# Queueing the S5 share behind the block's own work in the first stage of a hybrid encoder

## The chip, the cores and the metric

The kernel runs on one core of one Trainium2 chip. A core has a matrix engine (TensorE, PE in the rows), VectorE (DVE), ScalarE (ACT), GpSimd (POOL) and SyncE (SP); the last issues DMAs and computes nothing. Each engine takes its instructions in the order in which they stand in its own queue and waits on semaphores for the others. The metric is device time in microseconds (us) of one execution: the median of three runs before is 2523.85 us (2522.33 to 2524.93).

## The reference, cut to what matters

One layer, float32, on 3072 positions of width 1024 (one sequence of 1024, one of 2048):

```python
h = rmsnorm(x, norm_g)
u_a, v_a, z_a, x_b, z_b = split(h @ w_in)                 # five blocks of 1024 columns
y_a = gelu(u_a) * (w_s @ layernorm(gelu(v_a)) + b_s) * silu(z_a)       # chunks of 128 positions
y_b = S5 scan of x_b, forward and backward, 64 groups of 16 channels, 64 complex states each
y_b = glu(gelu(y_b + d_skip * x_b)) * silu(z_b)
out = rmsnorm(x + concat(y_a, y_b) @ w_out, final_g)
```

The S5 scan needs, for every group, matrices that come from the parameters alone (powers of the discretised state factor times the input and output maps). The kernel works these out itself: that is the "S5 setup".

## The kernel before, in words

Every float32 product is made of three passes over split operands (`mm3`, L57 to L61: high by high, high by low, low by high), so a block of 128 output columns by 512 positions is 24 matmuls of 512 columns.

**First stage (L204 to L365).** It makes x_b transposed, for three row groups `th` of 1024 positions. For each of them it runs 16 blocks: 8 weight columns times two halves of 512 positions, 48 blocks in all. A block is 24 matmuls `mm<-h..,whl` and then, in `xb_op`, one ScalarE copy of PSUM into the tile `xo` (L329); every second block SyncE sends `xo` out. After each block `after()` runs what else is due:

- a step of the norm of a coming half (`norm_half`). Its first step loads four tiles `x` of 128 rows, squares them on ScalarE (L267), works out the scale on tiny VectorE tiles (L269, and L48 to L53) and scales the four tiles on VectorE (L275). Each of the next eight steps is four TensorE transposes (`tr`, L283), a ScalarE copy `hf` (L285) and two VectorE passes, a cast and a subtraction (L287, L288), that leave a split tile of the half (`hx..`, `ha..`, `hb..`). A half has eight such tiles.
- from the third block on, a share of `s5_setup`. Blocks 3, 5, 7, 9 and 10 (the list `S5AT`, L34) take its head. From block 11 on every block takes one share: `build` of one pair of groups (32 pairs) and then `finish` of the pair before it.

A share's `build(gp)` (L953) is on VectorE two products, a difference and a scaled difference (`m`, `m`, `pc`, `pc`: L967, L968, L970, L972) and two products and a difference (L989, L990, L991: `pb`). GpSimd does the two products for the second `pc` (L967, L968), three operations for the second `pb` (L989 to L991) and four small copies into one of two tiles `Bm` (L997). ScalarE's queue issues four DMAs `mat_d<-pc` (L975). The share's `finish(gp - 1)` (L1000) is on TensorE four products into the PSUM tile `s5b` (L1007, eight rows in the trace) and four transposes into `s5a` (L1020). ScalarE copies `s5b` into `ksb` (L1010, L1011) and `s5a` into `pbt` (L1022). VectorE adds into `ksb` (L1012, the last reader of `s5b`) and finishes it (L1015, twice). ScalarE's queue sends both out (L1016, L1023). There is one `s5b` tile, so the `finish` of a pair can only start on TensorE when L1012 of the pair before is done.

Between blocks ScalarE and GpSimd also split the next weights `whl` (L151, L152: two halves for every weight, and a weight serves two blocks).

**The order.** The kernel is written in Python and a scheduler orders it when the program is built: it takes instructions by priority (the order of the text, moved by `tc.high_priority`) as soon as its own estimate says that their inputs are there, and puts them on the engines in that order. An instruction that the estimate finds ready may so be put ahead of older ones that are not. `with tc.issue_after(i.ins)` forbids that against one instruction: whatever is traced inside the block and goes to the same engine as `i` stands behind `i` in that engine's queue. It adds no wait across engines. The kernel uses it already for the first share of the setup, which is put behind the first half's scaling and copy:

```python
if blocks == S5AT[0]:
    with tc.issue_after(pin["x"].ins), tc.issue_after(pin["h"].ins):
        next(s5)
elif blocks in S5AT or blocks > S5AT[-1]:
    next(s5, None)
```

**Later stages (L368 on).** The second stage makes the other four column blocks, mixes branch A, and runs the 64 S5 groups in shares; the last two make the GLU and the output projection. Nothing in them is edited.

Of the kernel before, what the change touches and what calls it, by code (L numbers as in the profile page):

```python
# [11 lines left out]
F32 = mybir.dt.float32  # L12
# [4 lines left out]
ALU = mybir.AluOpType  # L17
# [16 lines left out]
S5AT = (3, 5, 7, 9, 10)  # L34
# [9 lines left out]
def newton_rsqrt(nc, pool, v, n, tag):  # L44

    y = pool.tile([P, n], F32, tag=tag + "y", name=tag + "y")
    a = pool.tile([P, n], F32, tag=tag + "a", name=tag + "a")
    nc.vector.tensor_scalar(y.bitcast(I32), v.bitcast(I32), -0.5, 1597463007.0,  # L48
                            op0=ALU.mult, op1=ALU.add)
    for _ in range(3):  # L50
        nc.vector.tensor_tensor(a, y, y, op=ALU.mult)
        nc.vector.scalar_tensor_tensor(a, a, -0.5, v, op0=ALU.mult, op1=ALU.mult)
        nc.vector.scalar_tensor_tensor(y, a, 1.5, y, op0=ALU.add, op1=ALU.mult)  # L53
    return y
# [9 lines left out]
def hybrid_encoder(ctx, tc, a, outs):  # L64
    nc = tc.nc
    V, S, G, T = nc.vector, nc.scalar, nc.gpsimd, nc.tensor
# [115 lines left out]
    def sweep(pool, half, ops, after, hp=WHP):  # L182

        ws = [ready.pop(0) for _ in ops]
        for jh in range(2):
            for w, f in zip(ws, ops):
                ps = pool.tile([P, 512], F32, tag="mm", name="mm")
                h = half(jh)
                for kt in range(KT):
                    mm3(nc, ps, w[:, 0, kt], w[:, 1, kt], h[kt][:, 0], h[kt][:, 1], kt == 0, kt == KT - 1)  # L190
                if jh:
                    next_w(hp)
                f(jh, ps)
                after()

    def by_j(t, jh):

        return t[:, :, 64 * jh:64 * jh + 64]

    def cols(t):  # L200
        return t.rearrange("p (k j) -> p j k", j=J)


    with ExitStack() as p1:  # L204
# [46 lines left out]
        pin = {}  # L251

        def norm_half(hf):


            th, jh = hf // 2, hf % 2
            ss = small.tile([P, 4], F32, tag="ss", name="ss")
            xs = []
            for c in range(4):
                if hf == 1:  # L260
                    x = hpool.tile([P, D], F32, tag=f"hb{c}", name="x")
                else:
                    x = xpool.tile([P, D], F32, tag="x", name="x")
                dma(x, x_src[th][P * (4 * jh + c):P * (4 * jh + c) + P])
                junk = xpool.tile([P, D], BF16, tag="junk", name="junk", bufs=1)
                with tc.issue_after(pin["h"].ins) if hf == 1 else ExitStack():
                    S.activation(junk, x, AF.Square, accum_out=ss[:, c:c + 1])  # L267
                xs.append(x)
            V.tensor_scalar(ss, ss, 1.0 / D, EPS, op0=ALU.mult, op1=ALU.add)  # L269
            rs = newton_rsqrt(nc, small, ss, 4, "rx")  # L270
            for c in range(4):
                if hf == 0 and c == 3:
                    pin["x0"] = S.activation(xs[c], xs[c], AF.Copy, scale=rs[:, c:c + 1])
                else:
                    pin["x"] = V.tensor_scalar(xs[c], xs[c], rs[:, c:c + 1], None, op0=ALU.mult)  # L275
            yield
            pool, tag = ((h1pool, "x"), (hpool, "a"), (hpool, "b"))[hf % 3]
            halves[hf] = []
            for kt in range(KT):
                h = pool.tile([P, 2, 512], F32R, tag=f"h{tag}{kt}", name=f"h{tag}{kt}")  # L280
                pt = ps_tr.tile([P, 512], F32, tag="tr", name="tr")
                for c in range(4):
                    T.transpose(pt[:, P * c:P * c + P], xs[c][:, P * kt:P * kt + P], ident)  # L283
                hf32 = xpool.tile([P, 512], F32, tag="hf", name="hf32", bufs=HFB)
                i = S.activation(hf32, pt, AF.Copy, scale=NG[:, kt:kt + 1])  # L285
                pin.setdefault("h", i)
                V.tensor_copy(h[:, 0], hf32)  # L287
                V.tensor_tensor(h[:, 1], hf32, h[:, 0].bitcast(F32), op=ALU.subtract)  # L288
                halves[hf].append(h)
                if hf < 4:  # L290
                    dma(hs_d[hf, kt], hf32)
                yield

        def steps(gen, n):
            for _ in range(n):
                next(gen, None)

        with tc.high_priority():
            n0 = norm_half(0)
            steps(n0, 1)  # L300

            stage_next()
            col = order.pop(0)[2]
            two = [hpool.tile([P, 512], F32, tag=f"hb{6 + i}", name="wf") for i in range(2)]
            src = w_in[:, col:col + P].rearrange("(kt p) c -> p kt c", p=P)
            for i in range(2):
                pin["w"] = dma(two[i].rearrange("p (a c) -> p a c", c=P), src[:, 4 * i:4 * i + 4])
            staged.append((None, two, lambda w: w))

            with tc.issue_after(pin["x0"].ins):  # L310
                split_w(1000)
                split_w(1000)
            steps(n0, 8)
        with tc.issue_after(pin["w"].ins):
            n1 = norm_half(1)
            steps(n1, 1)
            stage_next()
        s5 = s5_setup(p1, tc, a, xpool, ps_s5, ident, kio, f8h, f8l, r8, ks_d, mat_d)
        blocks = 0
# [3 lines left out]
        for th in range(NTH):  # L323
            xos = {}

            def xb_op(fb, jh, ps):
                if not jh:
                    xos[fb] = xpool.tile([P, J, P], F32, tag="xo", name="xo", bufs=2)
                S.copy(by_j(xos[fb][:, ::-1], jh), cols(ps))  # L329
                if jh:  # L330
                    dma(xb_d[P * fb:P * fb + P, :, P * th:P * th + P], xos[fb])

            def after():

                nonlocal blocks, n1, n2, n3
                i = blocks % 16
                if i < 2:
                    steps(n1, 2 if th else 4)
                if th < NTH - 1:
                    if i == 2:  # L340
                        n2 = norm_half(2 * th + 2)
                        steps(n2, 1)
                    if 4 <= i < 12:
                        steps(n2, 1)
                    if i == 12:
                        n3 = norm_half(2 * th + 3)
                        steps(n3, 1)
                    if i >= 14:
                        steps(n3, 2)
                    if i == 15:  # L350
                        n1 = n3
                blocks += 1
                if blocks == S5AT[0]:
                    with tc.issue_after(pin["x"].ins), tc.issue_after(pin["h"].ins):
                        next(s5)
                elif blocks in S5AT or blocks > S5AT[-1]:
                    next(s5, None)
                if blocks >= S5AT[-1]:
                    next(mx, None)

            for fbs in ((0, 1), (2,), (3,), (4,), (5,), (6, 7)):
                sweep(ps_mm, lambda jh: halves[2 * th + jh], [lambda *x, fb=fb: xb_op(fb, *x) for fb in fbs], after,
                      XHP if blocks else 0)
# [4 lines left out]
    with ExitStack() as p2:  # L368
# [8 lines left out]
        s5 = s5_groups(tc, spool, ps_b, small, kio, f8h, f8l, r8, xb_d, ks_d, mat_d, gy_d)  # L377
# [837 lines left out]
```

## Time and profile before

| what | value |
|---|---|
| median of three runs | 2523.85 us |
| profiled execution, its own time | 2522.37 us |
| its span, first to last instruction | 2520.6 us |
| TensorE busy | 2440.8 us, 97% of the span |
| VectorE busy | 1750.4 us, 69% |
| ScalarE busy | 976.7 us, 39% |
| GpSimd busy | 622.5 us, 25% |
| mean granted TensorE clock | 0.991 |
| first to last `xo` copy (the first stage's blocks) | 36.2 to 395.7 us |

The profiled execution took 1.8 us more than its span, and lies 1.5 us under the median. The shares of the whole span mix stages. The first stage is told apart by windows of time: in them "busy" of TensorE counts overlapping matmuls, so a window that reads 12.00 of 12.00 has no gap on TensorE, and what is missing to the window's length is time in which it waited.

### The profile page before, as it was taken

To read this page: it belongs to the slowest core of one execution; us is meant where nothing else is said; L and a number is where in the kernel's file an instruction comes from. 1 tells how busy PE (TensorE), PEld (TensorE's weight loads), DVE (VectorE), ACT (ScalarE), POOL (GpSimd) and SP (SyncE) were. 2 spreads that over 40 slices of the span, in tenths; PEclk is the share of its full clock that TensorE was granted. 3 is DMA by queue.
4 is the path that set the end of the run, shared out by engine and by line. 5 is a ranking of instruction groups with operands and counts; after the bars stand their busy time and mean duration, and the time that the engine had idled before them with its cause. 6 is when DMAs were issued, how large, how long until landed. Compare 5 with 4: busy or idle time off the path is not lost.

```text
span 2520.6 us, 34031 instructions
## 1 busy us (share of the span) xinstructions
PE 2440.8 (97%) x12313; PEld 2077.6 (82%) x12313; DVE 1750.4 (69%) x2921; ACT 976.7 (39%) x1738; POOL 622.5 (25%) x623
## 2 busy tenths in 40 slices
PE   7999999989999899999999999999999999999998
PEld 5777779978888798888889888887888888888886
DVE  6888856899999969888887989755455533333332
ACT  5343334445554534444454454424343411111110
POOL 1579873344334302210130231101000100000000
PEclk9999999999999999999999999999999999999999
DMA  8565455355555533544453444456465732222220
GB/s 240 171 190 146 143 161 192 115 170 175 177 181 190 179 100 122 153 157 149 135 177 119 127 132 150 135 168 179 135 183 160 234 109 92 92 96 93 96 76 30
DMA packets 363017, 367.21 MB, mean 146 GB/s; under 512 B 40768, under 2 KB 308576, under 8 KB 350560
## 3 DMA queue, kind: packets, MB, share of 16 engines
q1 hardware_dynamic: 311008, 343.99, 43.3%
q10 hardware_dynamic: 51840, 21.04, 3.4%
q8 instruction: 97, 1.59, 0.3%
q14 instruction: 72, 0.59, 0.1%
HBM read 229.76 MB, written 135.20 MB: 145 GB/s over the span
## 4 chain that ended last, share of the span: by engine, by line
PE 72%; DVE 12%; DMA 3%; issue 1%; POOL 1%; ACT 0%; SPq 0%; ACTq 0%; DVEq 0%; POOLq 0%
PE mm L59 20%; PE mm L61 20%; PE mm L60 19%; PE acc L59 2%; PE acc L60 2%; PE acc L61 2%; DVE gt L1121 2%; PE py L59 1%; PE py L61 1%; PE py L60 1%; PE sv L498 1%; DVE h L1127 1%; DMA hf<-hs_d 1%; PE pb L59 1%; PE pb L61 1%
## 5 line engine op out<-in xcount | busy, mean ns | idle before, releaser
L59 PE MATMUL mm<-w,yh 128*128 128x512 f32 x768 | 302.6, 394 | 0.0
L60 PE MATMUL mm<-w,yh 128*128 128x512 f32 x768 | 301.8, 393 | 0.0
L61 PE MATMUL mm<-w,yh 128*128 128x512 f32 x768 | 301.3, 392 | 0.0
L59 PE MATMUL mm<-ha,whl 128*128 128x512 f32 x704 | 277.7, 395 | 9.9 <-DVE v L503 9.6
L59 PE MATMUL mm<-hb,whl 128*128 128x512 f32 x704 | 277.5, 394 | 6.8 <-DVE v L503 6.8
L61 PE MATMUL mm<-ha,whl 128*128 128x512 f32 x704 | 275.6, 391 | 1.1 <-POOL whl L152 1.1
L61 PE MATMUL mm<-hb,whl 128*128 128x512 f32 x704 | 275.6, 391 | 0.0
L60 PE MATMUL mm<-ha,whl 128*128 128x512 f32 x704 | 275.4, 391 | 0.0
L60 PE MATMUL mm<-hb,whl 128*128 128x512 f32 x704 | 275.3, 391 | 0.0
L152 POOL TENSOR_TENSOR whl<-wf,whl 128x512 fp32r<-128x512 f32 x112 | 176.2, 1591 | 226.1 <-ACT whl L151 197.4
L1121 DVE TENSOR_TENSOR_SCAN gt<-dec,b 64x768 f32<-64x768 f32 x128 | 229.8, 1795 | 3.1
L1057 POOL TENSOR_TENSOR mi<-m,mi 128x256 fp32r<-128x256 f32 x64 | 59.7, 933 | 530.3 <-ACT mi L1056 530.3
L61 PEld LDWEIGHTS mm<-w,yh 128*128 128x128 f32 x768 | 144.3, 188 | 33.8
L59 PEld LDWEIGHTS mm<-w,yh 128*128 128x128 f32 x768 | 144.0, 188 | 33.2
L60 PEld LDWEIGHTS mm<-w,yh 128*128 128x128 f32 x768 | 144.0, 187 | 33.1
L700 DVE SCALAR_TENSOR_TENSOR yh<-yf,yh 128x512 fp32r<-128x512 f32 x96 | 66.8, 699 | 148.4 <-ACT yh L699 115.2
L59 PEld LDWEIGHTS mm<-ha,whl 128*128 128x128 f32 x704 | 132.9, 189 | 36.9 <-DVE v L503 10.4
L729 DVE TENSOR_TENSOR xr<-xr,mm 128x512 f32<-128x512 f32 x48 | 33.0, 688 | 184.1 <-PE mm L61 184.1
L59 PEld LDWEIGHTS mm<-hb,whl 128*128 128x128 f32 x704 | 133.1, 189 | 32.8 <-DVE v L503 7.7
L61 PEld LDWEIGHTS mm<-ha,whl 128*128 128x128 f32 x704 | 132.7, 188 | 29.4 <-POOL whl L152 1.6
L61 PEld LDWEIGHTS mm<-hb,whl 128*128 128x128 f32 x704 | 132.9, 189 | 27.9
L60 PEld LDWEIGHTS mm<-ha,whl 128*128 128x128 f32 x704 | 132.8, 189 | 25.9 <-DVE ha L288 0.4
(243 smaller groups left out, 5942.3 us busy)
## 6 DMA issues: line engine op xcount, KB each, us to landing
whl<-wc_d SPq DMA_DIRECT2D x64, 1024.0 KB
wc_d<-whl SPq DMA_DIRECT2D x32, 1024.0 KB
wf<-in_w_in_dram SPq DMA_DIRECT2D x112, 256.0 KB
m<-mat_d SPq DMA_DIRECT2D x128, 128.0 KB
xb_d<-xo SPq DMA_DIRECT2D x24, 512.0 KB
U<-xb_d SPq DMA_DIRECT2D x64, 192.0 KB
gy_d<-gy SPq DMA_DIRECT2D x64, 192.0 KB
zb_d<-zb SPq DMA_DIRECT2D x24, 512.0 KB
```

The source lines that it names most:

```text
L59: nc.tensor.matmul(out, lh, rh, start=first, stop=False)
L60: nc.tensor.matmul(out, lh, rl, start=False, stop=False)
L61: nc.tensor.matmul(out, ll, rh, start=False, stop=last)
L152: G.tensor_tensor(flat[:, 1, sl], wf, flat[:, 0, sl].bitcast(F32), op=ALU.subtract)
L498: T.matmul(sv[:, db], h[:, 0, dsl], w, start=True, stop=False)
L700: V.scalar_tensor_tensor(y[:, 1], yf, sc, y[:, 0].bitcast(F32), op0=ALU.mult, op1=ALU.subtract)
L729: V.tensor_tensor(x, x, t.ps[i], op=ALU.add)
L1057: eng.tensor_tensor(t[:, 1], src, t[:, 0].bitcast(F32), op=ALU.subtract)
L1121: V.tensor_tensor_scan(o[r, f], dec[r, f], bf[r, f], 0.0, op0=ALU.mult, op1=ALU.add)
L1127: V.tensor_tensor(h2, gt[:, ::-1], sn, op=ALU.mult)
```

## The change: what it does

From the eleventh block on, the share is traced under two `issue_after`: one for the last VectorE instruction of the block's own norm work (`pin["V"]`: a scaling L275 or a subtraction L288) and one for the block's ScalarE copy (`pin["S"]`: L329). The share's VectorE instructions then stand behind that scaling or subtraction on VectorE, and its ScalarE copies and its DMA issues from ScalarE's queue stand behind that `xo` copy. TensorE, GpSimd and SyncE get no such rule; the scheduler orders them anew around it. No instruction is added or taken away.

```diff
-                    pin["x"] = V.tensor_scalar(xs[c], xs[c], rs[:, c:c + 1], None, op0=ALU.mult)
+                    pin["x"] = pin["V"] = V.tensor_scalar(xs[c], xs[c], rs[:, c:c + 1], None, op0=ALU.mult)
...
-                V.tensor_tensor(h[:, 1], hf32, h[:, 0].bitcast(F32), op=ALU.subtract)
+                pin["V"] = V.tensor_tensor(h[:, 1], hf32, h[:, 0].bitcast(F32), op=ALU.subtract)
...
-                S.copy(by_j(xos[fb][:, ::-1], jh), cols(ps))
+                pin["S"] = S.copy(by_j(xos[fb][:, ::-1], jh), cols(ps))
...
-                elif blocks in S5AT or blocks > S5AT[-1]:
+                elif blocks in S5AT:
                     next(s5, None)
+                elif blocks > S5AT[-1]:
+
+                    with tc.issue_after(pin["V"].ins), tc.issue_after(pin["S"].ins):
+                        next(s5, None)
```

The queues of all five engines hold the same instructions as before, and up to the last block of the first stage they stand in another order: 214 rows on VectorE, 193 on ScalarE, 119 on GpSimd, 98 on TensorE and 3 on SyncE have moved. In the changed text, lines behind L358 have numbers that are higher by 4, so L1012 of before is L1016 there.

**VectorE, around the second share.** First before: `ksb_1233` belongs to the first pair, `pc_1311` to the third, `hb7` is a tile of the second half.

```order
L968 TENSOR_TENSOR m2_1310<-Ci_512,AO1_516 128x288
L244 TENSOR_SCALAR bs_1138<-bs_1138 128x512
L247 SCALAR_TENSOR_TENSOR RB_73<-tr_1136,fvec_69,bs_1138 128x128 x8
L970 TENSOR_TENSOR pc_1311<-m1_1309,m2_1310 128x288
L972 SCALAR_TENSOR_TENSOR pc_1319<-m1_1317,m2_1318 128x288
L989 TENSOR_TENSOR m1_1325<-Br_509,AI0_513 128x256
L287 CAST hb7_1185<-hf32_1191 128x512
L990 TENSOR_TENSOR m2_1326<-Bi_510,AI1_514 128x256
L288 TENSOR_TENSOR hb7_1185<-hf32_1191,hb7_1185 128x512
L1012 TENSOR_TENSOR ksb_1233<-ksb_1233,s5b_1228 16x2x16
```

The addition that frees `s5b` for the second pair stood behind most of the third pair's build. Now, around the same addition (`pc_1198` and `pc_1206` are the second pair's):

```order
L288 TENSOR_TENSOR hb7_1185<-hf32_1191,hb7_1185 128x512
L971 TENSOR_TENSOR m1_1196<-Cr_511,AO0_515 128x288
L972 TENSOR_TENSOR m2_1197<-Ci_512,AO1_516 128x288
L976 SCALAR_TENSOR_TENSOR pc_1206<-m1_1204,m2_1205 128x288
L974 TENSOR_TENSOR pc_1198<-m1_1196,m2_1197 128x288
L1016 TENSOR_TENSOR ksb_1233<-ksb_1233,s5b_1228 16x2x16
L993 TENSOR_TENSOR m1_1212<-Br_509,AI0_513 128x256
L994 TENSOR_TENSOR m2_1213<-Bi_510,AI1_514 128x256
L1019 SCALAR_TENSOR_TENSOR ksb_1233<-ident_93,dcol_517,ksb_1233 16x16
L995 TENSOR_TENSOR pb_1214<-m1_1212,m2_1213 128x256
```

The second pair's build stands behind the tile `hb7` now, and the addition stands inside that build, one share nearer to the front than before.

**TensorE, around the ninth pair's finish.** Before, at the border of two blocks (`hx` are tiles of one half, `hb` of the next; a block goes through the eight tiles of its half, and the last of `hx` is `hx_1799`, the first of `hb` `hb_734`):

```order
L59 MATMUL mm<-hx_1799,whl 128x512
L60 MATMUL mm<-hx_1799,whl 128x512
L61 MATMUL mm<-hx_1799,whl 128x512
L1007 MATMUL s5b<-pc,Bm_1049 48x144 x4
L1020 MATMUL s5a<-ident,pb 128x128 x4
L59 MATMUL mm<-hb_734,whl 128x512
```

The finish stood at the border. Now, after the block on `hb` that followed there, in the next block on `hx` (`hx_1476` and `hx_1487` are its first two tiles):

```order
L61 MATMUL mm<-hx_1476,whl 128x512
L59 MATMUL mm<-hx_1487,whl 128x512
L60 MATMUL mm<-hx_1487,whl 128x512
L1011 MATMUL s5b<-pc,Bm_1049 48x144 x4
L61 MATMUL mm<-hx_1487,whl 128x512
L1024 MATMUL s5a<-ident,pb 128x128 x4
L59 MATMUL mm<-hx_1586,whl 128x512
```

It stands after the fifth matmul of that block, one whole block further back.

**ScalarE, in the twelfth to fourteenth share.** Only the order now is shown; `ksb_2333` and `ksb_2431` are two pairs one after the other, `hf32_2390` the copy from which the block's VectorE passes are made.

```order
L979 DMA mat_d_64<-pc_2306 64x2x128
L1020 DMA ks_d_63<-ksb_2333 16x2x240
L329 COPY xo_2284<-mm_2348 128x8x64
L285 ACTIVATE hf32_2390<-tr_2385,fvec_69 128x512
L1026 COPY pbt_2443<-s5a_2438 128x512
L1027 DMA mat_d_64<-pbt_2443 128x2x256
L1014 COPY ksb_2431<-s5b_2426 16x2x128
L1015 COPY ksb_2431<-s5b_2426 16x2x112
```

The issue of `ks_d<-ksb` stands ahead of the next `xo` and `hf`, as it did before; what follows `xo` there is the share's own copies and DMA issues.

## Rows read from the trace of the kernel before

**Rows 1.** Busy time by stretch (us, then PE, PEld, DVE, ACT, POOL, clock, DMA, GB/s)
```profile
96.00:204.00 108.00, 97.53 (x479) 77.52 (x478) 93.80 (x183) 41.95 (x85) 86.57 (x123) 0.96 0.63 186
204.00:252.00 48.00, 47.67 (x251) 38.90 (x250) 37.11 (x73) 18.77 (x40) 45.63 (x62) 1.00 0.54 148
252.00:324.00 72.00, 65.84 (x345) 52.72 (x344) 60.35 (x123) 27.53 (x56) 60.53 (x85) 1.00 0.52 148
324.00:366.00 42.00, 41.98 (x211) 33.29 (x210) 22.31 (x51) 14.30 (x31) 36.97 (x55) 1.00 0.55 153
```

**Rows 2.** TensorE's waits from 96 to 400 us: total, times, longest
```profile
PE s5b L1007 <- DVE ksb L1012: 10.6, 8, 3.4
PE s5b L1007 <- DVE rxa L51: 3.4, 1, 3.4
PE tr L283 <- DVE x L275: 1.8, 4, 0.8
PE tr L241 <- DVE wsf L235: 0.6, 1, 0.6
PE mm L60 <- DVE hx L288: 0.4, 1, 0.4
```

**Rows 3.** Timeline of TensorE: start us, us, instruction, [idle before, releaser]
```profile
121.04 1.15 PE L1007 MATMUL s5b<-pc,Bm 128*48 128x144 f32 x8 [3.38 <-DVE ksb L1012]
182.89 1.47 PE L1007 MATMUL s5b<-pc,Bm 128*48 128x144 f32 x8 [3.41 <-DVE rxa L51]
193.25 1.15 PE L1007 MATMUL s5b<-pc,Bm 128*48 128x144 f32 x8 [1.13 <-DVE ksb L1012]
223.66 1.18 PE L1007 MATMUL s5b<-pc,Bm 128*48 128x144 f32 x8
231.26 1.18 PE L1007 MATMUL s5b<-pc,Bm 128*48 128x144 f32 x8
255.21 1.15 PE L1007 MATMUL s5b<-pc,Bm 128*48 128x144 f32 x8 [1.10 <-DVE ksb L1012]
281.32 1.15 PE L1007 MATMUL s5b<-pc,Bm 128*48 128x144 f32 x8 [1.44 <-DVE ksb L1012]
321.83 1.15 PE L1007 MATMUL s5b<-pc,Bm 128*48 128x144 f32 x8 [1.40 <-DVE ksb L1012]
```

**Rows 4.** Busy time by stretch, as rows 1: two that follow a long wait
```profile
120.00:132.00 12.00, 10.96 (x51) 8.93 (x52) 8.84 (x24) 6.75 (x13) 11.04 (x18) 0.86 0.63 194
180.00:192.00 12.00, 9.11 (x40) 7.33 (x40) 11.72 (x24) 3.87 (x10) 8.91 (x13) 0.86 0.71 200
```

**Rows 5.** Timeline of VectorE: the additions that release, the norm's scalings
```profile
120.73 0.17 DVE L1012 TENSOR_TENSOR ksb<-ksb,s5b 16x32 f32<-16x32 f32 x1
182.58 0.17 DVE L1012 TENSOR_TENSOR ksb<-ksb,s5b 16x32 f32<-16x32 f32 x1
266.07 0.20 DVE L269 TENSOR_SCALAR ss<-ss 128x4 f32<-128x4 f32 x1 [1.33 <-ACT junk L267]
268.28 2.74 DVE L275 TENSOR_SCALAR x<-x,rxy 128x1024 f32<-128x1024 f32 x4
```

**Rows 6.** Timeline of ScalarE: first and last square of one norm; one block's copies
```profile
224.21 0.33 ACTq L1016 DMA_DIRECT2D ks_d<-ksb  x1
225.88 0.59 ACT L329 COPY xo<-mm 128x512 f32<-128x512 f32 x1 [5.79 <-PE s5a L1020]
226.36 0.70 ACT L285 ACTIVATE hf<-tr,fvec 128x512 f32<-128x512 f32 x1
252.02 1.06 ACT L267 ACTIVATE junk<-x 128x1024 bf16<-128x1024 f32 x1 [0.45 <-ACT pbt L1022]
```

**Rows 7.** Timeline of VectorE and GpSimd: one operation with and without a neighbour
```profile
250.62 2.76 POOL L152 TENSOR_TENSOR whl<-wf,whl 128x512 fp32r<-128x512 f32 x2
250.69 1.53 DVE L972 SCALAR_TENSOR_TENSOR pc<-m,m 128x288 f32<-128x288 f32 x1 [1.27 <-POOL m L968]
259.72 0.46 DVE L972 SCALAR_TENSOR_TENSOR pc<-m,m 128x288 f32<-128x288 f32 x1 [2.08 <-POOL m L968]
```

## The prediction, made before the run

> **What bounds the kernel now.** I read the busy times by stretch first. In the reader's place, look at how much of each stretch TensorE fills: 97.53 of 108 us from 96 to 204, 47.67 of 48 from 204 to 252, 65.84 of 72 from 252 to 324, 41.98 of 42 from 324 to 366 [rows 1]. TensorE is the bound, and the two stretches with gaps are those in which the norm of a coming half and a share meet. The list of waits then gives the gaps a name: 10.6 us in 8 waits of `s5b` for the addition L1012, 3.4 us of `s5b` put down to `rxa`, 1.8 us of transposes for scaled `x`, 0.6 and 0.4 us of others [rows 2]. The wait put down to `rxa` is one for L1012 too: its finish starts at 182.89, and an addition ends at 182.58 + 0.17 = 182.75 [rows 3, 5]. Together TensorE waits 16.8 us. The timeline of TensorE shows the large ones singly: 3.38, 3.41, 1.13, 1.10, 1.44, 1.40 [rows 3].
>
> Two of them cost more than their length. In the stretches that hold the waits of 3.38 and 3.41 us the granted clock is 0.86, where it is 1.00 from 204 on [rows 1, 4]. Of the two levels, 1.2 and 2.4 GHz, the lower is half the upper, so 0.14 / 0.5 x 12 us = 3.4 us ran at half rate, and half of that, some 1.6 us, is lost behind each long wait. All that the change could win on TensorE is thus 16.8 + 2 x 1.6 = 20.0 us.
>
> **The change part by part.** No instruction is added or removed, so there is no work to add up; what counts is where L1012 and the finish stand. Before, VectorE does the addition of one pair behind most of the build of the next pair but one. After, it stands inside the next pair's build, and TensorE's finish comes up to a block later. The two shifts act alike: the release is asked for earlier on VectorE and needed later on TensorE. Against them stands that the build now waits for the block's scaling or subtraction, which it used to run ahead of.
>
> *The first finishes.* The wait of 3.38 us at 121.04 ends with an addition that VectorE had put behind the third pair's build [rows 3, 5]. With the addition in the second build, and the second finish asked for where it was, it is ready in time: 3.4 us and the clock's 1.6, so +5.0 us (plus is gain). The wait for `wsf` of 0.6 us [rows 2] is for VectorE work on the mixing weights that shared its queue with the early builds, and these now stand later: +0.6.
>
> *The third finish.* The four waits for scaled `x`, 1.8 us, are of the transposes behind a norm [rows 2]; VectorE had share work ahead of the scalings, and the scalings now go first: +1.8. But the second pair's addition is then behind the four scalings and half a build. The nearest row for the scalings is 2.74 us, for a build's operation 0.46 [rows 5, 7]; the four operations ahead of it make about 1.9. I charge the third finish, which the new order puts right behind the transposes, with 2.5 us of new wait: bounds are 0 (if the later place on TensorE covers it) and 2.74 + 1.9 = 4.6. Net -0.7.
>
> *The ninth and tenth.* The second norm has waits of 3.41 and 1.13 us and 1.6 us of clock, 6.1 in all. Here the ninth finish goes a whole block back on TensorE, but the addition also goes behind the scalings. Of the same 4.6 us the block and five matmuls more on TensorE cover most for the ninth, and I keep 1; the tenth follows only some 20 matmuls later, so I keep 3 of 4.6. Net 6.1 - 4 = +2; bounds 6.1 (no new wait) and -1 (4.6 for one of them, 2.5 for the other).
>
> *The steady blocks from 204 to 252* have no wait of 1 us. The small one of 0.3 us there and the 0.4 us of `hx` may go: +0.7. What may come is below, in the first rival; in the sum I keep -2 for it.
>
> *The third norm.* The waits of 1.10 and 1.44 us [rows 3] belong here, and 1.8 of the 2.1 us that the three smaller of the eight make (10.6 less the 8.45 of the five shown): 4.4. After, the addition of the eighteenth pair stands behind the scalings (268.28 + 2.74 = 271.0, then four operations of the build: 273) and the nineteenth finish is asked for at about 263 + 7.6 = 270.6 [rows 5]; it waits about 2.2, the next 0.5. Net +1.7. The block's period of 7.6 us is the distance of two finishes without a wait, 223.66 to 231.26 [rows 3].
>
> *Behind the third norm* there are no norm steps, the pinned instruction is long done, and little is reordered; the 1.40 us at 321.83 stay [rows 3]: 0. TensorE is full from 324 to 366 [rows 1], so nothing is to be had there. The later stages keep their order on every engine: 0.
>
> The sum: 5.0 + 0.6 - 0.7 + 2 + 0.7 - 2 + 1.7 = 7.3 us. Against the profiled execution, 2522.4 us, that is 2515.1. The median of the runs is 1.5 us higher, 2523.85, so the forecast is 2516.6, in round figures 2517 us.
>
> ScalarE's rule moves no wait that I can see: the share's `ks_d` issue takes 0.33 us, stands ahead of `xo` before and after, and ScalarE has 5.79 us of idle time ahead of `xo` [rows 6]: 0, unless the loop of the first rival closes through it.
>
> **The rivals.** *First, slower: the loop VectorE, ScalarE, VectorE becomes longer than the block.* Where a block has norm passes, its build now waits for the subtraction, that for `hf`, that for `xo` and the issue of `ks_d` ahead of it in ScalarE's queue, and that issue for VectorE's last operation of the share before. Per block ScalarE's part is 0.33 + 0.59 + 0.70 = 1.62 us [rows 6], VectorE's 37.11 / 48 x 7.6 = 5.9 us [rows 1]: 7.5 us against 7.6. Nothing is left over. Before, VectorE could fill the time in which it waits for `hf` with the build; now it can't. Any stretching beyond today's makes each block late: one operation of the build takes 1.53 us where a GpSimd split `whl` of 2.76 us lies beside it, and 0.46 where none does [rows 7], so one more meeting costs 1.07 us. Over some 14 shares whose block has norm passes this is up to 15 us of lag, and half of that if every second meeting exists today; with nothing left over I take 12, nearer the upper end. Less the 7.3 gained that is +4.7: 2528.5 against the median. It decides as soon as the loop exceeds 7.6 us by 0.5 a block. For it: the sum has no room. Against it: ScalarE's and VectorE's parts overlap in part, and the build's stretched operations may come out of the way of `whl`.
>
> The Trainium skill, on its page "SBUF — State Buffer", section "Who interferes with whom", says that a VectorE instruction with two SBUF inputs contends with a GpSimd instruction that reads SBUF, and in the strict case the one that issues second is blocked until the first is done. The 1.53 against 0.46 us agree with it in direction. By full blocking a meeting would cost up to the 2.76 us of the split instead of 1.07, and the first rival would be worth some 10 us more.
>
> *Second, no change: the waits only move.* At each of the three norms the addition that was late behind a build is late behind the scalings instead, at the bounds above: 4.6 at the third finish, 4.6 + 2.5 at the ninth and tenth, 4.6 at the nineteenth, 16.3 us in place of the 9.2 that the sum holds (2.5 + 4 + 2.7). Its 7.3 us shrink to 0.2: 2523 to 2524. For it: the scalings' chain (the last square, then the tiny operations 266.07 to 268.28, then 2.74 us) is fixed by ScalarE [rows 5, 6], and from the first square of that norm, at 252.02, to the first tiny operation, which waits for the last square until 266.07, 14 us pass, in which the pinned builds can't run ahead. Against it: TensorE's finishes are moved back as well.
>
> *Third, all waits go.* The later places on TensorE cover the later additions, and the loop stays short: 7.3 + 9.2 + 2 = 18.5 us at the most, 2505, and 2505 to 2511 as a case. Against it: it needs every guess above at its good end.
>
> **How the numbers follow.** I give the forecast 0.40, the second rival 0.28, the first 0.20, the third 0.12. A measurement of this kernel tells about 0.2% from no change, that is 5 us: below 2518.8 counts as faster, above 2528.9 as slower. The forecast's own range is 2511 to 2520, 0.33 of its 0.40 being faster, and 0.07 the same. The second rival is mostly the same (0.23), with 0.02 faster and 0.03 slower; the first 0.18 slower and 0.02 the same; the third 0.12 faster. Together 0.47 faster, 0.32 the same, 0.21 slower. The range of 8 in 10 is 2507 to 2530: it leaves out the best part of the third rival and the worst of the first.
>
> **What would show it.** Right: no wait of 3 us for L1012 (by its new number L1016) near 121 and 183, the granted clock there near 1.00 instead of 0.86, new waits of 1 to 3 us behind the scalings of each norm, and the last `xo` copy some 7 us earlier than 395.7. The first rival would show as waits of TensorE from 204 to 252, where there is next to none now, with TensorE's busy time below 46 of 48 us and ScalarE's `hf` late. The second would show as 15 us or more of waits in the list, at other places. My step is wrong if the waits of the later stages change, since I took them as fixed, or if the transposes still wait for scaled `x`.

## The result: 32 us slower, all of it in the first stage

| | before | changed |
|---|---|---|
| median of four runs | 2524.39 us | 2556.26 us (2552.25 to 2564.31) |
| ratio | 1 | 1.0131 (95% interval 1.0115 to 1.0147) |
| span of the profiled execution | 2520.6 us | 2553.8 us |
| mean granted TensorE clock | 0.991 | 0.984 |
| last `xo` copy | 395.65 us | 428.56 us |

The forecast was 2517 us, with a range from 2507 to 2530. The last `xo` copy is 32.9 us late and the span 33.2 us longer: all of the loss is made in the first stage.

Two numbers account for it. The list of TensorE's waits from 96 to 430 us of the changed kernel (total, times, longest) answers to [rows 2]:

```profile
PE s5b L1011 <- DVE ksb L1016: 20.9, 8, 7.5
PE s5a L1024 <- DVE pb L995: 12.0, 14, 1.3
PE tr L283 <- DVE x L275: 2.7, 7, 0.7
PE s5a L1024 <- DVE ksb L1019: 1.1, 1, 1.1
```

That is 36.7 us against 16.8, so 19.9 more, and 12.0 us of it is of a kind that before doesn't have: the finish's transposes `s5a` wait for `pb` of the build. The busy times by stretch answer to [rows 1]; the figure to read is the clock, third from the end:

```profile
96.00:204.00 108.00, 94.58 (x442) 73.18 (x441) 78.55 (x159) 38.36 (x78) 66.33 (x105) 0.95 0.58 175
204.00:252.00 48.00, 42.02 (x214) 33.56 (x215) 34.97 (x70) 16.93 (x35) 35.98 (x59) 0.96 0.43 121
252.00:324.00 72.00, 63.25 (x306) 50.63 (x305) 51.77 (x106) 24.85 (x50) 47.36 (x74) 0.91 0.49 142
324.00:366.00 42.00, 33.25 (x156) 26.33 (x155) 31.23 (x59) 13.41 (x28) 33.61 (x52) 0.92 0.41 112
366.00:400.00 34.00, 34.00 (x174) 27.08 (x173) 17.00 (x36) 9.71 (x21) 23.93 (x35) 1.00 0.58 166
```

At half rate in part of a stretch, the time lost is (1 - clock) x length: 5.4 + 1.9 + 6.5 + 3.4 = 17.2 us here, and 4.3 before (0.96 in the first stretch alone), so 12.9 more. Waits and clock together make 32.8 us of 33.2; as the clock is given to 0.01, its part is good to about 1 us.

The timeline of TensorE shows where (start, us, instruction, [idle before, releaser]), as [rows 3] did:

```profile
117.38 1.18 PE L1011 MATMUL s5b<-pc,Bm 128*48 128x144 f32 x8
134.92 2.13 PE L1011 MATMUL s5b<-pc,Bm 128*48 128x144 f32 x8 [1.32 <-DVE ksb L1016]
145.80 2.16 PE L1011 MATMUL s5b<-pc,Bm 128*48 128x144 f32 x8 [2.69 <-DVE ksb L1016]
206.65 2.13 PE L1011 MATMUL s5b<-pc,Bm 128*48 128x144 f32 x8 [3.84 <-DVE ksb L1016]
254.52 0.63 PE L1024 MATMUL s5a<-ident,pb 128*128 128x128 f32 x4 [0.90 <-DVE pb L995]
304.65 1.30 PE L1011 MATMUL s5b<-pc,Bm 128*48 128x144 f32 x8 [2.69 <-DVE ksb L1016]
345.41 2.13 PE L1011 MATMUL s5b<-pc,Bm 128*48 128x144 f32 x8 [7.48 <-DVE ksb L1016]
```

The 3.38 us that a finish waited at 121.04 are gone, as forecast (117.38 has no idle time). The 3.41 us near 183 are gone, but 3.84 stand at 206.65, 2.69 at 145.80 and 304.65, and 7.48 at 345.41, in a place (the 25th finish) where the kernel before goes on without a wait:

```profile
313.19 1.18 PE L1007 MATMUL s5b<-pc,Bm 128*48 128x144 f32 x8
```

**The loop.** Two engines of the changed kernel between 245 and 256 us, in the steady stretch. ScalarE (`ACTq` are its DMA issues):

```profile
246.41 0.33 ACTq L1020 DMA_DIRECT2D ks_d<-ksb  x1
246.79 0.59 ACT L329 COPY xo<-mm 128x512 f32<-128x512 f32 x1
247.27 0.70 ACT L285 ACTIVATE hf<-tr,fvec 128x512 f32<-128x512 f32 x1
251.50 3.25 ACTq L979 DMA_DIRECT2D mat_d<-pc  x4
255.04 0.35 ACTq L1020 DMA_DIRECT2D ks_d<-ksb  x1
255.43 0.59 ACT L329 COPY xo<-mm 128x512 f32<-128x512 f32 x1 [5.74 <-DMA mat_d<-pc]
```

VectorE:

```profile
245.67 0.67 DVE L1019 SCALAR_TENSOR_TENSOR ksb<-ident,dcol,ksb 16x16 f32<-16x16 f32 x1
248.00 0.51 DVE L287 CAST ha<-hf 128x512 fp32r<-128x512 f32 x1 [1.66 <-ACT hf L285]
248.55 0.69 DVE L288 TENSOR_TENSOR ha<-hf,ha 128x512 fp32r<-128x512 f32 x1
253.97 0.41 DVE L995 TENSOR_TENSOR pb<-m,m 128x256 f32<-128x256 f32 x1
254.30 0.66 DVE L1019 SCALAR_TENSOR_TENSOR ksb<-ident,dcol,ksb 16x16 f32<-16x16 f32 x1
```

VectorE's last operation of a share ends at 245.67 + 0.67 = 246.34. The issue of `ks_d` has stood in ScalarE's queue for it and goes at 246.41, `xo` at 246.79, `hf` at 247.27; VectorE has idled 1.66 us when the cast starts at 248.00, the build follows the subtraction, and the next share ends at 254.30 + 0.66 = 254.96. The round took 8.62 us; the one ahead of it (from 238.83) 7.51. TensorE's own block takes 7.6 [rows 3]. At the next turn `ks_d` goes at 255.04 and `xo` at 255.43, with ScalarE idle for 5.74 us before it, though TensorE had begun the transposes behind that block at 251.91. (At 246.79 `ks_d` was not alone: two `whl` splits of ScalarE that end at 246.69 would have held `xo` as long.) The four issues of `pc` stand in the same queue ahead of `ks_d` and end at 251.50 + 3.25 = 254.75, so they hold it nearly as long as VectorE does. Before, a share's last operation stood right behind the block's subtraction and the builds of later pairs behind it, so `ks_d` was out well before `xo` was due (224.21 and 225.88 in [rows 6]), and the loop had slack. In VectorE's queue the addition of a pair stood behind the start of the third build counted from its own pair; now it stands behind the start of the second, until the norm passes end (from the 24th pair on it is the third and then the fourth). VectorE has lost a lead of one build, so each `pb` comes at the moment when TensorE asks for it (the 14 waits of `s5a`).

**The norms.** The waits of VectorE and GpSimd from 96 to 400 us, changed kernel:

```profile
DVE ss L269 <- ACT junk L267: 22.1, 3, 8.8
...
```

```profile
POOL m L993 <- DVE pc L976: 66.4, 19, 13.5
...
```

VectorE stands 22.1 us in front of the norms' squares (2.1 before), since the builds that filled this time stand behind the scalings. GpSimd waits 66.4 us (19.5 before) for the `pc` that lets go its product tile.

### The profile page after: what moved, and what is told of

Read it like the earlier page. It is cut to its first block, busy times and chain, and to the rows that moved or that the text cites. A ratio compares the mean times of both kernels' runs of the same rounds, so it can differ in the third digit from the quotient of the medians.

```text
span 2553.8 us, 33929 instructions
## 1 busy us (share of the span) xinstructions
PE 2456.1 (96%) x12313; PEld 2087.0 (82%) x12313; DVE 1750.6 (69%) x2921; ACT 978.1 (38%) x1738; POOL 602.2 (24%) x623
## 4 chain that ended last, share of the span: by engine, by line
PE 76%; DVE 11%; DMA 2%; issue 1%; POOL 1%; ACT 1%; ACTq 0%; SPq 0%; DVEq 0%; POOLq 0%
PE mm L59 20%; PE mm L61 20%; PE mm L60 20%; PE acc L59 3%; PE acc L60 3%; PE acc L61 3%; DVE gt L1125 2%; PE py L59 1%; PE py L61 1%; PE py L60 1%; PE sv L502 1%; DMA whl<-wc_d 1%; PE pb L59 1%; PE pb L61 1%; PE pb L60 1%
## 5 line engine op out<-in xcount | busy, mean ns | idle before, releaser
L60 PEld LDWEIGHTS mm<-w,yh 128*128 128x128 f32 x768 | 144.0, 187 | 32.9
```

The lines of the kernel that those rows point to most:

```text
L60: nc.tensor.matmul(out, lh, rl, start=False, stop=False)
```

## The experiments

Beside the totals, the start of TensorE's blocks tells where a kernel loses time. The table gives the start of the last matmul `mm` of blocks 14, 19, 22, 29, 35 and 48 (for the kernel before in us, for the others less that of the kernel before; each from one trace). At these six matmuls all eight kernels have begun the same number of finishes. Between blocks 14 and 19 lie the norm behind the first shares and blocks with two tiles of the half, 19 to 22 holds the second norm, 22 to 29 are the steady blocks with one tile, 29 to 35 holds the third norm and blocks with two tiles; behind 35 there is no norm work.

| kernel | 14 | 19 | 22 | 29 | 35 | 48 | median, us |
|---|---|---|---|---|---|---|---|
| before, start in us | 129.44 | 171.93 | 200.09 | 253.72 | 305.69 | 393.50 | 2524.4 |
| changed | -4.7 | +6.5 | +9.4 | +14.1 | +23.4 | +32.8 | 2556.3 |
| older mark (`e7`) | -5.7 | +0.2 | +3.9 | +3.5 | +5.9 | +7.8 | 2533.7 |
| addition too (`e9`) | -6.8 | +4.8 | +5.5 | +11.3 | +20.4 | +30.0 | 2557.4 |
| before, addition (`e8`) | -5.5 | -1.6 | -2.9 | +1.5 | +7.2 | +8.4 | 2535.2 |
| no scalings (`e10`) | -4.7 | +4.6 | +11.2 | +13.5 | +20.9 | +29.1 | 2553.8 |
| issues put off (`e20`) | -4.8 | +1.5 | +3.2 | +3.0 | +7.5 | +18.0 | 2543.5 |
| put off, no scalings (`e21`) | -6.2 | -2.5 | -1.0 | -1.4 | -0.5 | +10.5 | 2534.4 |

**Which rule, which part.** Four kernels take the change apart: VectorE's rule alone, ScalarE's alone, both rules on the build alone, both on the finish alone.

```diff
-with tc.issue_after(pin["V"].ins), tc.issue_after(pin["S"].ins):
+with tc.issue_after(pin["V"].ins):        # e1; e2: pin["S"] alone
...
 cur = build(gp)
+yield      # the rules hold up to here (e3), or from here on (e4)
 if last:
```

> Only the rule for VectorE; ScalarE's is left out. Theory A (VectorE's rule takes away the lead of one build that VectorE had over the finishes, so pb and the addition come late): the loss stays almost whole, 2548 to 2560 us, with s5b waits of 15 us or more, 8 to 12 us of s5a waits for pb, and clocks under 0.9 in several stretches between 130 and 350 us. Rival B (ScalarE's rule puts the copies of s5b and the four issues of pc behind the block's xo, and through them the addition): under 2532 us. Rival C (both are needed): about half, 2533 to 2546.

> Only the rule for ScalarE. Theory A: VectorE keeps its lead (in the queue the addition of a pair stands behind the start of the third or fourth build after it, as before), so within 8 us of before, 2518 to 2532, and next to no s5a wait for pb. Rival B: 2545 or more, with ScalarE's copies of s5b late. Rival C: 2533 to 2546.

> Both rules, but only for the build part of a share; the finish (its copies, its additions, its sends) is free. Theory A: the lead is lost by the build's place, so as slow as the changed kernel, 2546 to 2560. Rival B (the finish's ScalarE copies are what is late): under 2535.

> Both rules, but only for the finish part of a share; the build is free to run ahead. Theory A: near before, 2518 to 2532, with s5a not waiting for pb. Rival B: the copies of s5b and the addition are late as in the changed kernel, 2540 or more.

Measured: VectorE's rule alone 2557.4 us, ratio 1.0131 (1.0110 to 1.0152); ScalarE's alone 2527.2, 1.0005 (0.9993 to 1.0017); the build alone 2556.7, 1.0121 (1.0098 to 1.0145); the finish alone 2532.8, 1.0036 (1.0022 to 1.0051). TensorE's waits with VectorE's rule alone, then with ScalarE's alone:

```profile
PE s5b L1011 <- DVE ksb L1016: 21.6, 8, 7.5
PE s5a L1024 <- DVE pb L995: 14.1, 13, 2.5
```

```profile
PE s5b L1011 <- DVE ksb L1016: 14.7, 9, 5.3
PE s5b L1011 <- DVE rxy L53: 2.6, 1, 2.6
```

The first has both kinds of wait, the second none for `pb`. Theory A holds: VectorE's rule, on the build, makes the whole loss by itself. ScalarE's rule alone costs nothing that is clear of noise. Both rules on the finish alone cost 8.2 us, a little more than theory A allowed (2532.8 against at most 2532); beside the rule on the build they add nothing.

**Giving the lead back.** The mark is taken from one block earlier; ScalarE's rule stays.

```diff
-with tc.issue_after(pin["V"].ins), tc.issue_after(pin["S"].ins):
+with tc.issue_after(pin.get("V0", pin["V"]).ins), tc.issue_after(pin["S"].ins):
     next(s5, None)
+pin["V0"] = pin["V"]
```

> The changed kernel, with VectorE's rule made one block older: the share stands behind the last scaling or subtraction of the block before, not of its own; ScalarE's rule is kept. In VectorE's queue the addition of a pair again stands behind the start of the third build counted from its own pair, as before the change, in most shares. Theory A (what costs is the lost lead of one build, not the rule as such): 2518 to 2534, no row of s5a waiting for pb with more than 3 us. Rival D (any build held behind norm passes costs, by the scalings at the three norms): 2538 or more.

2533.7 us, 1.0040 (1.0025 to 1.0055): 23 of the 32 us come back, and the list has no wait for `pb`. So most of the cost comes with the lost lead, and not with a build's standing behind norm passes at all; 9.3 us stay.

**Rules on the addition, and a second `s5b` tile.** The prediction took the late addition for the thing to mend. Three runs took it up directly.

```diff
+pin["A"] = V.tensor_tensor(ksb[...], ksb[...], pk[...], op=ALU.add)
...
+with tc.issue_after(pin["A"].ins):        # e8: kernel before; e9: changed kernel
     next(s5, None)
```

```diff
-ps_tr = p1.enter_context(tc.tile_pool(name="ps_tr", bufs=3, space=PSUM))
+ps_tr = p1.enter_context(tc.tile_pool(name="ps_tr", bufs=2, space=PSUM))
-pk = ps.tile([48, 2, 144], F32, tag="s5b", name="s5b")
+pk = ps.tile([48, 2, 144], F32, tag="s5b", name="s5b", bufs=2)
```

> The changed kernel, and the build of every share also stands behind the addition of the share before it on VectorE, so that VectorE can't run two builds ahead of an addition when the norm passes end (near 345 us in the changed kernel). Theory A with its second part (the 7.5 us wait there is VectorE taking its lead back in front of an addition; with half rate behind it some 10 us): 2543 to 2550. If the wait there is made by GpSimd or ScalarE instead: within 4 us of the changed kernel, 2552 to 2560.

> The kernel before, with one rule alone: from the second share on a build stands behind the addition of the share before it on VectorE; nothing stands behind the norm passes. The lead stays at two builds and each addition comes one build earlier. Theory A: the waits for the addition before the change (14 us, and 3 us of half rate) get less and no new wait comes: 2508 to 2520, faster than before. Rival E (the additions were late for their copies on ScalarE or for the norm's squares, not for the build ahead): 2521 to 2529.

> The kernel before with two s5b tiles and two instead of three tr tiles (PSUM is full). A finish then waits for the addition of the pair before the last. If the addition is what TensorE waits for: the 14 us of s5b waits go to under 4, 2508 to 2518, unless the third tr tile is needed, which would show as transposes waiting for hf by 5 us or more and 2524 to 2535.

The changed kernel with the rule on the addition: 2557.4, 1.0129 (1.0116 to 1.0142), no gain. The 7.48 us at 345 are gone, but:

```profile
PE s5b L1012 <- DVE ksb L1017: 19.7, 13, 3.8
```

13 waits of at most 3.8 us make nearly the same sum; behind block 35 it loses 9.6 us where the changed kernel loses 9.4. VectorE's queue of the changed kernel shows how the wait at 345 came about:

```profile
341.91 0.46 DVE L976 SCALAR_TENSOR_TENSOR pc<-m,m 128x288 f32<-128x288 f32 x1 [2.78 <-POOL m L972]
345.09 0.17 DVE L1016 TENSOR_TENSOR ksb<-ksb,s5b 16x32 f32<-16x32 f32 x1
```

The addition stands behind two builds, and one of them waits 2.78 us for a product of GpSimd. That order made this one wait, but the second part of theory A, that the loss goes with it, is refuted. The kernel before with the same rule: 2535.2, 1.0039 (1.0026 to 1.0052), slower, where I expected a gain. The lead did not stay at two builds, as I had expected: in VectorE's queue every addition but the last stands behind the start of the second build, as in most of the changed kernel. Without a rule on norm passes this costs 10.8 us. With two `s5b` tiles the kernel before runs 2525.4, 1.0004 (0.9995 to 1.0012):

```profile
PE tr L283 <- DVE x L275: 6.2, 6, 3.7
PE s5a L1020 <- ACT pbt L1022: 4.4, 2, 3.7
PE tr L241 <- DVE wsf L235: 2.3, 1, 2.3
```

No wait for the addition is left, and the time is the same: others, 6.2, 4.4 and 2.3 us, took its place (with one `tr` tile less, which may have a part in them). The 20 us that the prediction took for the upper bound of a gain did not come with an `s5b` that is never waited for; what a second `s5b` tile gives with all three `tr` tiles was not run.

**The norms and GpSimd.** Theory F said that the loss is made at the norms, and kept because GpSimd has no time to spare.

```diff
-pin["x"] = pin["V"] = V.tensor_scalar(...)           # e10: only subtractions are marks
+pin["x"] = V.tensor_scalar(...)
...
-m1 = wp.tile(sh, F32, tag=f"m1{i}", name="m1", bufs=1)      # e11, e13; m2 alike
+m1 = wp.tile(sh, F32, tag=f"m1{i}", name="m1", bufs=1 + i)
...
-G.tensor_copy(bm[r, i, :, 32 * d:32 * d + 16], bt[r, gs])    # e12
+S.copy(bm[r, i, :, 32 * d:32 * d + 16], bt[r, gs])
```

> The changed kernel, but VectorE's rule takes only the subtractions of the norm blocks (L288) as its mark, not the scalings (L275): where a norm begins, the share stands behind the last subtraction of an earlier block and may run while ScalarE squares. Theory F (the loss is made at the three norms: VectorE and, through the products' tiles, GpSimd stand idle there, 20 us of VectorE's wait for the squares and one GpSimd wait of 13.5 us, and the time is not made up later because GpSimd has little spare): 2524 to 2540. Rival G (the hold behind the subtraction of every block costs as much): 2543 to 2556.

> The changed kernel with two instead of one of GpSimd's two product tiles in the build (m1, m2 of its half), and nothing else: the order on all engines stays as in the changed kernel. GpSimd may then go on with the products for pb while VectorE has not yet read those for pc. Theory F: GpSimd's 66 us of waiting for pc shrink to under 30, and the kernel gains, 2530 to 2548. Rival H (VectorE's own place in the order is all that counts, GpSimd is only dragged along): 2550 to 2560.

> The changed kernel with the four small copies into Bm on ScalarE instead of GpSimd, some 37 us of GpSimd's time in the first stage. Theory F (GpSimd has too little spare to make up the holds): 2532 to 2548. Rival H: 2550 or more, since VectorE's order stays nearly as it is.

> The kernel before with two of GpSimd's product tiles, order unchanged. GpSimd waits 19.5 us there for VectorE's pc and VectorE 27 us for GpSimd's products. Theory F: VectorE's builds come earlier, the additions too, and some of TensorE's 14 us of waits go: 2512 to 2521. Otherwise 2522 to 2527, no change.

2553.8 (1.0118, 1.0105 to 1.0132), 2554.7 (1.0122, 1.0109 to 1.0136) and 2557.7 (1.0128, 1.0113 to 1.0144): none gains more than 2.5 us. Theory F falls as an account of the whole loss. Without the marks at the scalings the loss stands in nearly the same places. The kernel before with two product tiles is slower, 2531.5, 1.0029 (1.0018 to 1.0041); its list has one wait of 7.4 us for `wsf` at the start of the shares, which I don't explain.

**Which loop.** Two loops could hold the blocks: S, through ScalarE's queue as shown above, and T, through TensorE, where the next block stands behind transposes that wait for `pb`. T is opened by a finish one share later (three tiles of `pc`, `pb`, `Bm`, two `hf`), S by issues from SyncE.

```diff
-    cur = build(gp)
-    if last:
-        finish(*last)
-    last = cur
+    last.append(build(gp))
+    if len(last) > 2:
+        finish(*last.pop(0))
...
-dma(ks_d[gs].rearrange("g c o -> c g o"), ksb)      # those of mat_d alike
+nc.sync.dma_start(ks_d[gs].rearrange("g c o -> c g o"), ksb)
```

> The changed kernel with the finish one more share behind the build (build of pair k, then finish of pair k - 2), three instead of two pc, pb and Bm tiles, and two hf tiles instead of three to make room. Each finish on TensorE then finds its pb a whole share earlier; the build still stands behind the block's subtraction, and the issue of ks_d still ahead of xo and hf in ScalarE's queue. Loop T (tr, hf, subtraction, build, pb, the finish's transposes on TensorE, and so the next block) is what makes each block late: 2520 to 2538. Loop S (the last VectorE operation of a share, the issue of ks_d on ScalarE, xo, hf, subtraction, build): 2545 or more.

> The changed kernel with the share's DMAs (mat_d and ks_d) issued by SyncE instead of ScalarE, so that no issue that waits for VectorE stands ahead of xo and hf. Loop S: 2520 to 2540, with hf within 2 us of its transposes. Loop T: 2545 or more, and s5a waits for pb stay at 10 us or more. A cost of its own: SyncE's loads of wf and x stand behind issues that wait, which would show as split weights late.

> Both of the last two edits on the changed kernel: the finish one share later, and the share's DMAs on SyncE. If the two loops S and T are the whole of the loss: 2516 to 2532. If it stays above 2540 neither is, and the place of the builds behind the norms is what is left.

> The kernel before with the finish one more share behind the build, and the same tiles as the first of these runs: its control. If the tiles and the later finish cost nothing by themselves: 2515 to 2530. Above 2535 the first of these runs can't be read by itself, only against this one.

2561.2 us (1.0149, 1.0133 to 1.0166), 2563.1 (1.0151, 1.0136 to 1.0166), 2570.7 (1.0182, 1.0167 to 1.0197), and the control, 2543.0 (1.0071, 1.0049 to 1.0092). With the later finish TensorE's list reads:

```profile
PE s5b L1011 <- DVE ksb L1016: 28.9, 14, 8.9
PE s5a L1024 <- DVE pb L995: 0.9, 2, 0.5
```

The waits for `pb` are nearly gone, 0.9 us instead of 12.0, but those for the addition are 8.0 us longer, and the kernel is no faster: T alone does not set the pace. The control costs 20 us by itself, so the first run has to be read against it, as was said beforehand: 2561.2 against 2543.0, 18 us instead of the change's 32. A part of the loss may thus hang on T; these runs do not settle it. The runs with SyncE tell nothing about S, since they make another wait, seen on ScalarE of the first:

```profile
240.62 0.36 ACT L1014 COPY ksb<-s5b 16x256 f32<-16x256 f32 x1 [7.15 <-DMA ks_d<-ksb]
```

The copy into `ksb` waits 7.15 us for the send of `ksb` before it: SyncE issues that behind its loads, and there is one `ksb` tile.

**Opening loop S alone.** ScalarE keeps the issues; those of `pc` and `ksb` of a share are put off to the next share, behind that block's `xo` and `hf`, and `ksb` has two tiles instead of one. `pin["H"]` is the last `hf` copy.

```diff
+def send():
+    with tc.issue_after(pin["H"].ins):
+        for x in late:
+            dma(*x)
+    late.clear()
...
-        dma(ks_d[gs].rearrange("g c o -> c g o"), ksb)
+        late.append((ks_d[gs].rearrange("g c o -> c g o"), ksb))
```

> The changed kernel; the issues of mat_d<-pc and ks_d<-ksb of a share are put off to the next share and stand behind that block's xo and hf in ScalarE's queue (two ksb tiles instead of one). By then VectorE is done with them, so no issue that waits for VectorE stands ahead of xo and hf. Loop S (share's last VectorE operation, issue of ks_d, xo, hf, subtraction, build): the blocks with norm passes come down to TensorE's own period, 2530 to 2546. If the loss is instead that VectorE simply has no work between a block's border and its hf, whoever is ahead of hf: 2548 to 2560.

> The same, and VectorE's rule leaves out the scalings as its mark (as in the run that did that alone and came out at 2554). If loop S was what kept that run slow, and the holds at the norms are the rest: 2522 to 2538. If neither: 2546 or more.

2543.5 us, 1.0069 (1.0054 to 1.0085), and without the marks at the scalings 2534.4, 1.0041 (1.0026 to 1.0056). In the first of them, ScalarE in a steady block:

```profile
241.92 0.59 ACT L330 COPY xo<-mm 128x512 f32<-128x512 f32 x1 [2.06 <-PE mm L61]
242.40 0.69 ACT L285 ACTIVATE hf<-tr,fvec 128x512 f32<-128x512 f32 x1
245.48 0.55 ACTq L1036 DMA_DIRECT2D ks_d<-ksb  x1
```

`xo` and `hf` go when TensorE is done, and `ks_d` behind them. TensorE's finishes there follow each other after 7.6 us (234.66 and 242.25 us). Between blocks 22 and 29 the changed kernel loses 4.7 us and this one gains 0.2, though its lead is still one build. So loop S is what made the steady blocks late. Loop T was left as it was, and yet TensorE waits only 2.1 us for `pb`, where the changed kernel has 12.0:

```profile
PE s5a L1025 <- DVE pb L996: 2.1, 4, 0.9
```

Two things in the edit were not tried alone. The issues of `ks_d` and of `pc` were put off together, so the runs do not tell how much each of them held. And the second `ksb` tile could have helped by itself, since ScalarE of the changed kernel waits for the send of the only one:

```profile
ACT ksb L1014 <- DMA ks_d<-ksb: 14.8, 10, 3.5
```

In the steady blocks, though, this delays VectorE's addition just once, by 0.28 us at 218.93.

With the scalings out of the rule too, the kernel is level with before up to block 35 (-0.5 us): with the loop closed that edit was worth 2.5 us of the median, with the loop open 9.1. Both holds were there, and the loop hid the other. Together they account for the changed kernel's +23.4 us at block 35: 15.9 go with the loop and 8.0 more with the scalings.

Behind block 35 the two lose 10.5 and 11.0 us, more than the changed kernel (9.4), and there the cause is the putting-off itself. VectorE of the second:

```profile
349.56 0.46 DVE L975 TENSOR_TENSOR pc<-m,m 128x288 f32<-128x288 f32 x1 [7.60 <-DMA mat_d<-pc]
```

A build waits 7.60 us for its `pc` tile to be sent, and the addition right behind it lets TensorE's finish at 351.04 wait 3.36 us; there are 6 such waits of VectorE, 21.2 us together. A kernel with both edits up to the last norm and the old order behind it was not run; by the one trace at block 35 it could be about as fast as before. No version run here beats the kernel before.

## Why the prediction was wrong, step by step

| stretch (TensorE's blocks) | the forecast's gain | measured gain | issues put off (`e20`) | and no scalings (`e21`) |
|---|---|---|---|---|
| up to 14: the first finishes and `wsf` | +5.6 | +4.7 | +4.8 | +6.2 |
| 14 to 19: third finish | -0.7 | -11.2 | -6.2 | -3.7 |
| 19 to 22: ninth and tenth | +2 | -2.9 | -1.7 | -1.6 |
| 22 to 29: steady blocks | +0.7 - 2 | -4.7 | +0.2 | +0.5 |
| 29 to 35: third norm | +1.7 | -9.2 | -4.5 | -0.9 |
| 35 to 48: behind the norms | 0 | -9.4 | -10.5 | -11.0 |

- *The first finishes* were right in kind and nearly in size: the wait at 121.04 and its half rate went.
- *The loop* is the step that failed. The text worked it out as 7.5 us against a block of 7.6, said that nothing was left over, and then kept -2 us for it in the sum and a chance of 0.20 for the rival. The loop measured 7.5 and 8.6 us in turn, the longer one where an operation stands beside a `whl` split, and the sign named for it came: TensorE busy for 42.02 of 48 us from 204 to 252. What opening it gives back is 15.9 us up to block 35, and not in the steady blocks alone, but also where the blocks have two tiles (14 to 19 and 29 to 35). The first rival had the mechanism and its trigger; its 12 us were too small, and the sum should have gone by it: a loop as long as the block has no room for one late meeting. The text's loop also leaves out the four issues of `pc`, 3.25 us of ScalarE's queue in the share shown above. Two of the rival's figures don't hang together either: its +4.7 takes the whole sum of 7.3 from the 12, though the -2 in that sum is for the same loop (without it, 12 - 9.3 = +2.7); and 2528.5 lies below 2528.9, so that most of the rival should have counted as the same, not as slower.
- *The norms* (third finish, ninth and tenth, third norm). Their new waits were priced by what stands ahead of the addition in its queue, 4.6 us at most. What came besides is that VectorE has nothing to do before the squares (22.1 us) and then owes that work to the blocks that follow. With the loop open, the marks at the scalings cost 8.0 us up to block 35 (`e20` against `e21`). An engine that is held behind a mark loses work, not only one reply.
- *Half rate* was counted for the two waits that go and for none that come. It makes 12.9 of the 33 us.
- *Behind the norms* I had 0, as little is reordered there. Nearly all of the 9.4 us of this stretch stand at the 7.48 us at 345.41 and the half rate around it; behind it TensorE loses nothing more. I read them as a debt: the builds arrive there late, and spreading the waits (`e9`) pays none of it back (9.6 us), while the kernel before with the same rule, whose builds stand behind no norm pass, loses 1.2 there (`e8`). That it is a debt is not shown, and what sets the pace while it is paid was not settled: GpSimd is busy 33.6 of the 42 us from 324 to 366, but taking its copies away (`e12`) gained nothing.
- *ScalarE's rule* was rightly put at nothing by itself (1.0005).
- *The late addition* as the thing worth mending was probably wrong for the kernel before, too: with no wait for it at all (`e6`) the time is the same, though with one `tr` tile less.

What a meeting of VectorE and GpSimd costs was right. VectorE, then GpSimd, of the changed kernel:

```profile
242.03 0.45 DVE L972 TENSOR_TENSOR m<-Ci,AO 128x288 f32<-128x288 f32 x1
249.55 1.54 DVE L972 TENSOR_TENSOR m<-Ci,AO 128x288 f32<-128x288 f32 x1
```

```profile
249.39 1.38 POOL L152 TENSOR_TENSOR whl<-wf,whl 128x512 fp32r<-128x512 f32 x1
```

The second product takes 1.54 us instead of 0.45 and ends at 251.09, 0.3 us after the split does (250.77). The Trainium skill, page "SBUF — State Buffer", section "Who interferes with whom", has the second of the two blocked until the first is done; that agrees nearly here, and with the 1.53 us of [rows 7], if the block there lasted for the first of two splits that take 2.76 us together. The prediction's other price, 2.76 us, took the two for one.

## What to carry to other kernels

Before an engine's filler work is ordered behind a step of the main loop, follow the ring that this closes (here VectorE, a waiting DMA issue in ScalarE's queue, two ScalarE copies, VectorE) and compare its length with the period: here, about equal was already too long. A lead in an in-order queue is a resource; an order that makes a late reply earlier by giving up that lead can trade one wait for small ones in many blocks. And when one wait among several is taken away, ask who is next: in `e6` the whole wait for `s5b` was gone, other waits stood in its place, and the time had not moved.

## What the runs showed of the hardware that was not expected

Short waits in a busy stretch came with a lower clock. In the changed kernel the granted clock is 0.91 from 252 to 324 us and 0.92 from 324 to 366, a part of the time at the lower of the two levels, where before it was 1.00, with the engine still busy 88% and 79% of these stretches: 9.8 us on top of the waits there. And a DMA issue that waits for a semaphore in ScalarE's queue holds the copies behind it: `xo` of the block behind which TensorE's transposes began at 251.91 us went at 255.43, 0.39 us after `ks_d`, with ScalarE idle for 5.74 us before it.
